# Low halves of two weight products by ScalarE and an adding DMA instead of VectorE, in a down projection by seven products

## The chip, the cores and the metric

The kernel runs on one core of one Trainium2 chip. The metric is device microseconds of one execution, the median of several runs. A run varies by about 0.1%: three runs of the kernel before took 2109.35 to 2111.09 us.

TensorE multiplies; VectorE (DVE in the profile), ScalarE (ACT) and GpSimd (POOL) prepare its operands; SyncE (SP) issues most DMAs. PEld in the profile is TensorE's load of the stationary operand, which overlaps its matmuls (PE).

## The reference

Two layers, each with two SwiGLU half-steps around a mixer of a gated linear recurrence and windowed attention. Everything is float32. What matters here is the last product of the SwiGLU, which happens four times (two per layer):

```python
def swiglu(h, w_gate, w_up, w_down):
    return (jax.nn.silu(h @ w_gate) * (h @ w_up)) @ w_down

for l in range(DEPTH):                     # 2 layers, 512 tokens, D_MODEL 1024, D_FF 2816
    h = rms_norm(x, gn[0])
    x = x + 0.5 * rms_norm(swiglu(h, w_ffn1_gate[l], w_ffn1_up[l], w_ffn1_down[l]), gn[1])
    ...
    h = rms_norm(x, gn[4])
    x = x + 0.5 * rms_norm(swiglu(h, w_ffn2_gate[l], w_ffn2_up[l], w_ffn2_down[l]), gn[5])
```

## The kernel before

**Precision.** A float32 product is made of three matmuls in a reduced float32 format. Each operand is split into a high half (the value rounded) and a low half (the rest); `mm3` adds high x high, high x low and low x high. So every weight that TensorE reads has first been split: ScalarE casts it into the high half `whi`, and the low half `wlo` is the weight minus the high half. There are two ways to make a low half:

- VectorE subtracts: `wlo = w - whi` (L286 in `quarter`, L331 in `split`).
- ScalarE writes `-w` rounded into `wlo` (L283, L328), and a DMA issued by GpSimd adds the float32 `w` onto it (L284, L329). Activations have the same two ways in `split` (L400 and L401) and `split_dma` (L410, L411, L412).

**Weights in a stream.** `Stream` holds the order in which weights are used. `load` fetches a unit of 128 x 1024 float32 into one of 4 raw buffers (`w`, tag w32), by SyncE. A unit's next load waits until all readers of the old contents are done. `split` and `quarter` make high and low halves into 6 buffers each (`whi`, `wlo`), up to three items ahead of the one in use. Whatever TensorE does is in program order; the other engines' instructions are put in order when the program is built, and each engine then runs its list strictly in that order.

**The down projection.** `down` multiplies 22 row blocks of 128 with the down weights, tokens on the output's partitions. Most of it runs in units of 256 rows (`both`). For rows 8 to 15 of the first half of the columns it uses `quarters`: a 2 x 2 block product by **seven products** of sums of the blocks instead of eight. Their order is `ORDER`: p1, p6, p2, p7, p5, p4, p3. Each product takes two weight items (index q = 0, 1), each of 128 x 1024 in two halves of 512 columns, and runs 2 items x 2 row blocks x 2 token blocks x 3 matmuls = 24 matmuls of 128x512. The matmul of one row block reads columns out of both halves of its item.

**Where the weights of a product come from.** `quarter(it)` does it: p1 and p5 read raw units 0 and 1, p2 and p4 read raw units 2 and 3, before and after these are changed; p6, p7 and p3 read sums that VectorE makes:

- p6: L267 subtracts in raw units 0 and 1 in place, L268 writes a second difference (`tt`).
- p7: L276 adds in the buffers of the second column half, and L277 adds `tt` **in place into raw units 2 and 3**, the same that p2 has read and p4 will read.

These sums are pinned: they stay in program order on VectorE. After p5 and p4 a raw unit is given back (`raw.pop`) and the next load into that buffer is queued on SyncE.

The names that recur: `x56` and `x37` in `Late` are the activations' sums for the products 5, 6 and 3, 7. The ones for product 7 and 3 are split by `late.more` through `split` (L400, L401) and `split_dma` (L410 to L412). `u2`, `u3`, `c12` and `c22` (L789) add up the products on VectorE. L799 copies p1 out of PSUM by ScalarE.

The tail of `quarter`, L278 to L286, which decides on the way of the low half:

```python
for c in range(2):
    nc.scalar.copy(it.hi[:, h[c]], w[c])                                             # L281
    if it.kind in DMAS:
        nc.scalar.mul(it.lo[:, h[c]], w[c], -1.0)                                    # L283
        nc.gpsimd.dma_start(it.lo[:, h[c]].bitcast(F32), w[c], accum_op=ALU.add)     # L284
    else:
        nc.vector.tensor_tensor(it.lo[:, h[c]], w[c], it.hi[:, h[c]].bitcast(F32), op=ALU.subtract)  # L286
```

Of the kernel before, what the change touches and what calls it, by code (L numbers as in the profile page):

```python
# [37 lines left out]
TURN = 0  # L38
LEAD = 8
ORDER = ("p1", "p6", "p2", "p7", "p5", "p4", "p3")  # L40
DMAS = ()
HEADS = (0, 4, 1, 5, 2, 6, 3, 7)


# [1 line left out]
def trunk(ctx: ExitStack, tc: tile.TileContext, xin, wall, gains, lbT, hgain, sinks, c_dist, c_mask, c_ident, out):  # L46
# [109 lines left out]
    class Stream:  # L156
# [98 lines left out]
        def quarter(self, it):  # L255
# [24 lines left out]
# [4 lines that stand above are left out]
# [1160 lines left out]
```

## Time and profile before

| | us |
|---|---|
| median of 3 runs | 2109.81 |
| lowest, highest | 2109.35, 2111.09 |
| the profiled execution, its own time | 2112.72 |
| its span, first to last instruction | 2110.9 |

The page gives busy time by engine, and the groups of instructions by line. Rows of a timeline read: start in us from the span's start, duration in us, engine, line, operation, output<-input, shape, count; in brackets the idle time of the engine before it and what ended it. A row with "x4" is four instructions one behind the other, and its duration is that of all four. Rows of one line's answer give min, median and max duration in ns, and below it who waited for that line (us, times). DMA rows give queue, packets, MB and the share of 16 DMA engines, or issues with size and us from the issue's start to landing.

The four down projections by seven products lie at about 260 to 303, 958 to 1001, 1304 to 1346 and 2002 to 2045 us.

### The profile page before, as it was taken

Reading aid. Unit: us, or ns where it says so; the run is one execution under the profiler, and the core shown is the slowest. Engines: PE = TensorE matmul, PEld = TensorE weight load, DVE = VectorE, ACT = ScalarE, POOL = GpSimd, SP = SyncE. Lnnn points to the kernel's source line nnn. Section 1 sums busy time; section 2 is a strip of 40 time slices with the busy share of each in tenths; the row PEclk is TensorE's granted clock in tenths of the full one; section 3 lists DMA queues with packets and bytes.
Section 4 is the critical chain, followed back from the end, with each engine's and each line's share of the span. In section 5 each row is a group of like instructions: output and inputs, shape, how many; then the busy total and the mean of one; then the engine's idle time right before and its main releaser. Section 6 shows DMA issues by size and latency. Waiting matters only on the chain.

```text
span 2110.9 us, 35242 instructions
## 1 busy us (share of the span) xinstructions
PE 2100.8 (100%) x13549; PEld 1874.8 (89%) x13549; DVE 1551.3 (73%) x2705; ACT 1122.6 (53%) x1899; POOL 154.6 (7%) x188
## 2 busy tenths in 40 slices
PE   9999999999999999999999999999999999999998
PEld 8899988887888999997899998898778989999987
DVE  5877886767676777789587778767686758777884
ACT  6555555446444555556355556444554445555562
POOL 0011000000000011110001110000000000111000
PEclk9999999999999999999999999999999999999999
DMA  8677653322246357774447775632122563677651
GB/s 246 152 181 182 175 167 123 101 70 65 66 110 200 127 122 182 180 195 126 151 113 176 185 179 147 190 119 91 51 71 70 135 187 108 157 182 183 179 163 47
DMA packets 148072, 298.36 MB, mean 141 GB/s; under 512 B 16992, under 2 KB 74816, under 8 KB 147904
## 3 DMA queue, kind: packets, MB, share of 16 engines
q1 hardware_dynamic: 122416, 228.16, 33.2%
q0 software_dynamic: 25344, 67.91, 18.6%
q8 instruction: 106, 1.74, 0.3%
q14 instruction: 62, 0.51, 0.1%
q10 hardware_dynamic: 144, 0.05, 0.0%
HBM read 213.43 MB, written 14.73 MB: 108 GB/s over the span
## 4 chain that ended last, share of the span: by engine, by line
PE 44%; DVE 6%; ACT 3%; issue 1%; DMA 1%; SPq 0%; ACTq 0%; DVEq 0%
PE acc L115 32%; PE aux L115 11%; ACT whi L324 1%; DVE s L401 1%; DMA w<-wall 1%; DVE wlo L286 1%; DVE wlo L331 1%; PE aux L125 1%; PE acc L125 0%; ACT s L400 0%; SPq L241 0%; DVE tt L268 0%; DVE w L267 0%; ACT m L894 0%; ACT whi L281 0%
## 5 line engine op out<-in xcount | busy, mean ns | idle before, releaser
L115 PE MATMUL acc<-s,whi 128*128 128x256 f32 (+1 forms) x4952 | 1063.0, 311 | 0.4 <-ACT whi L324 0.2
L115 PEld LDWEIGHTS acc<-s,whi 128*128 128x128 f32 x4952 | 806.2, 191 | 51.5 <-DVE s L1101 1.6
L115 PE MATMUL acc<-s,wlo 128*128 128x256 f32 (+1 forms) x2476 | 766.9, 310 | 0.1
L115 PEld LDWEIGHTS acc<-s,wlo 128*128 128x128 f32 x2476 | 472.5, 191 | 25.5 <-DVE wlo L331 0.4
L324 ACT CAST whi<-w 128x1024 fp32r<-128x1024 f32 (+1 forms) x341 | 317.1, 949 | 254.0 <-PE aux L115 95.0
L115 PE MATMUL acc<-whi,s 128*128 128x512 f32 x1264 | 414.0, 394 | 0.3 <-ACT s L400 0.2
L324 ACT CAST whi<-tt 128x1024 fp32r<-128x1024 f32 x154 | 161.6, 1049 | 342.2 <-DVE tt L318 189.2
L331 DVE TENSOR_TENSOR wlo<-w,whi 128x1024 fp32r<-128x1024 f32 (+1 forms) x181 | 218.5, 1216 | 134.0 <-ACT whi L324 133.0
L115 PEld LDWEIGHTS acc<-whi,s 128*128 128x128 f32 x1264 | 236.9, 188 | 57.6 <-issue 3.2
L331 DVE TENSOR_TENSOR wlo<-tt,whi 128x1024 fp32r<-128x1024 f32 x154 | 188.2, 1222 | 103.0 <-ACT whi L324 102.7
L115 PE MATMUL acc<-wlo,s 128*128 128x512 f32 x632 | 246.8, 391 | 1.2 <-DVE wlo L286 1.2
L329 POOL DMA_DIRECT2D wlo<-w x160 | 138.2, 865 | 1263.0 <-ACT wlo L328 869.1
L115 PE MATMUL aux<-s,whi 128*128 128x256 f32 (+1 forms) x1248 | 230.5, 285 | 0.0
L115 PE MATMUL aux<-whi,s 128*128 128x512 f32 x592 | 196.8, 390 | 0.0
L115 PEld LDWEIGHTS aux<-s,whi 128*128 128x128 f32 x1248 | 195.2, 192 | 1.1 <-issue 0.5
L115 PE MATMUL aux<-s,wlo 128*128 128x256 f32 (+1 forms) x624 | 177.6, 285 | 0.0
L115 PEld LDWEIGHTS acc<-wlo,s 128*128 128x128 f32 x632 | 118.7, 188 | 25.7 <-DVE wlo L286 2.4
L115 PEld LDWEIGHTS aux<-whi,s 128*128 128x128 f32 x592 | 111.1, 188 | 22.9
L328 ACT ACTIVATE wlo<-w 128x1024 fp32r<-128x1024 f32 (+1 forms) x160 | 130.0, 846 | 0.0
L400 ACT CAST s<-s 128x512 fp32r<-128x512 f32 (+1 forms) x164 | 88.5, 581 | 65.9 <-DVE s L459 60.6
L115 PEld LDWEIGHTS aux<-s,wlo 128*128 128x128 f32 x624 | 119.8, 192 | 0.5 <-DMA wlo<-w 0.2
L115 PE MATMUL aux<-wlo,s 128*128 128x512 f32 x296 | 115.2, 389 | 0.0
(186 smaller groups left out, 2136.6 us busy)
## 6 DMA issues: line engine op xcount, KB each, us to landing
w<-wall SPq DMA_DIRECT2D x267, 512.0 KB, 3.7
wlo<-w POOLq DMA_DIRECT2D x83, 512.0 KB, 5.5
w<-wall SPq DMA_DIRECT2D x288, 128.0 KB, 3.2
wlo<-w POOLq DMA_DIRECT2D x77, 256.0 KB, 3.3
x_d<-s SPq DMA_DIRECT2D x48, 256.0 KB, 2.1
s<-x_d SPq DMA_DIRECT2D x48, 256.0 KB, 5.3
w<-wall SPq DMA_DIRECT2D x34, 256.0 KB, 3.0
s<-wall SPq DMA_DIRECT2D x64, 128.0 KB, 3.5
```

The lines of the kernel that those rows point to most:

```text
L115: nc.tensor.matmul(o, lhsT, rhs, start=start, stop=stop)
L125: nc.tensor.transpose(o, src, ident)
L286: nc.vector.tensor_tensor(it.lo[:, h[c]], w[c], it.hi[:, h[c]].bitcast(F32), op=ALU.subtract)
L324: i = nc.scalar.copy(it.hi[:, c], w[:, c])
L328: nc.scalar.mul(it.lo[:, c], w[:, c], -1.0)
L329: nc.gpsimd.dma_start(it.lo[:, c].bitcast(F32), w[:, c], accum_op=ALU.add)
L331: nc.vector.tensor_tensor(it.lo[:, c], w[:, c], it.hi[:, c].bitcast(F32), op=ALU.subtract)
L400: nc.scalar.copy(hi, src)
L401: nc.vector.tensor_tensor(lo, src, hi.bitcast(F32), op=ALU.subtract)
```

## The change

Products p2 and p4 make their low halves by ScalarE and an adding DMA; the other five stay with VectorE. The whole diff is the list that `quarter` asks:

```diff
 ORDER = ("p1", "p6", "p2", "p7", "p5", "p4", "p3")
-DMAS = ()
+DMAS = ("p2", "p4")
 HEADS = (0, 4, 1, 5, 2, 6, 3, 7)
```

For each of the four down projections, 8 subtractions of 128x512 on VectorE (L286) are replaced by 8 scaled copies of 128x512 on ScalarE (L283) and 8 adding DMAs of 256 KB issued by GpSimd (L284).

## The prediction

> **What bounds the kernel now.** I read the busy shares first, then who waited for the two weight-splitting lines of the seven products, then one of the four places instruction by instruction.
>
> ```profile
> span 2110.9 us, 35242 instructions
> ...
> PE 2100.8 (100%) x13549; PEld 1874.8 (89%) x13549; DVE 1551.3 (73%) x2705; ACT 1122.6 (53%) x1899; POOL 154.6 (7%) x188
> ```
>
> TensorE sets the time; VectorE, with 73%, and ScalarE, with 53%, matter only where TensorE waits for them. So the question is where in the four down projections TensorE waits, and how the change moves those waits. Who waited for the high halves (L281) and for VectorE's low halves (L286):
>
> ```profile
> L286 DVE TENSOR_TENSOR wlo<-w,whi x64: 680/686/694, 243.3 to 2031.1; 128x512 fp32r<-128x512 f32 x64
> ...
>   PEld acc L115: 2.4, 4
> ...
> L281 ACT CAST whi<-w x64: 614/618/627, 241.3 to 2027.5; 128x512 fp32r<-128x512 f32 x64
> ...
>   PEld acc L115: 1.4, 4
> ```
>
> Each line stopped the weight loads four times, once per down projection: 2.4 + 1.4 = 3.8 us in all, 0.95 us a place. Both stops are in one product, shown here for the first place (TensorE's rows: the first matmul of p6, p2, p5 and p4; then the two stopped weight loads, inside p7):
>
> ```profile
> 269.10 0.39 PE L115 MATMUL aux<-whi,s 128*128 128x512 f32 x1
> 274.54 0.39 PE L115 MATMUL acc<-whi,s 128*128 128x512 f32 x1
> 286.22 0.39 PE L115 MATMUL aux<-whi,s 128*128 128x512 f32 x1
> 291.66 0.39 PE L115 MATMUL acc<-whi,s 128*128 128x512 f32 x1
> ...
> 282.80 0.19 PEld L115 LDWEIGHTS acc<-whi,s 128*128 128x128 f32 x1 [0.36 <-ACT whi L281]
> 283.60 0.19 PEld L115 LDWEIGHTS acc<-wlo,s 128*128 128x128 f32 x1 [0.61 <-DVE wlo L286]
> ```
>
> A product is 24 matmuls: 274.54 - 269.10 = 5.44 us, 0.227 us each, 2.72 us for each of its two weight items. p2 runs 274.54 to 279.98; p7 then reaches its second item at 282.7 and loses 0.95 us there. ScalarE and VectorE around it:
>
> ```profile
> 270.37 2.18 ACT L281 CAST whi<-w 128x512 fp32r<-128x512 f32 x4
> 273.41 0.62 ACT L400 CAST s<-s 128x512 fp32r<-128x512 f32 x1
> 274.45 0.63 ACT L411 ACTIVATE s<-s 128x512 fp32r<-128x512 f32 x1
> 274.98 0.61 ACT L400 CAST s<-s 128x512 fp32r<-128x512 f32 x1
> 276.96 0.62 ACT L281 CAST whi<-s 128x512 fp32r<-128x512 f32 x1 [0.31 <-DVE s L276]
> 282.66 3.22 ACT L281 CAST whi<-w 128x512 fp32r<-128x512 f32 x6
> 285.78 2.19 ACT L281 CAST whi<-s 128x512 fp32r<-128x512 f32 x4
> ...
> 271.11 2.49 DVE L286 TENSOR_TENSOR wlo<-w,whi 128x512 fp32r<-128x512 f32 x4
> 274.06 0.69 DVE L401 TENSOR_TENSOR s<-s,s 128x512 fp32r<-128x512 f32 x1 [0.47 <-ACT s L400]
> 275.63 0.69 DVE L401 TENSOR_TENSOR s<-s,s 128x512 fp32r<-128x512 f32 x1 [0.87 <-ACT s L400]
> 276.24 0.69 DVE L276 TENSOR_TENSOR s<-s,s 128x512 f32<-128x512 f32 x1
> 282.26 1.29 DVE L286 TENSOR_TENSOR wlo<-s,whi 128x512 fp32r<-128x512 f32 x2
> 284.66 4.90 DVE L286 TENSOR_TENSOR wlo<-w,whi 128x512 fp32r<-128x512 f32 x8
> ```
>
> The chain that ends in TensorE's stop, read backwards: p7's last low halves (282.26 to 283.55) close a string of VectorE work that began with the first L276 at 276.24 and has no gap. That L276 stands behind two L401, and both waited for **ScalarE's** L400 (0.47 and 0.87 us idle). So up to 275.6 ScalarE is late, not VectorE. The four subtractions that the change takes away (271.11 to 273.60) lie ahead of those idle gaps.
>
> **The change part by part.** For p2 and p4 each place loses 2 x 4 VectorE subtractions and gains 2 x 4 scaled copies on ScalarE (L283) and 2 x 4 adding DMAs of 256 KB on GpSimd (L284). In the order in which the changed program is built, TensorE's instructions are unchanged; p2's copies stand one behind each of its four L281, p4's four stand behind the first of p3's L281; the two L401 still stand ahead of the first L276.
>
> *p2's subtractions removed:* 2.49 us of VectorE. Worth 0: L401 waits for ScalarE. Below nothing they cannot go far: the cover of a gain is the 0.95 us stop in p7, 3.8 us in four places.
>
> *p2's scaled copies:* the twin is L411, which starts at 274.45 and lets L400 start at 274.98, 0.53 us. Four make 2.12 us, and all four lie between the L281 at 270.37 and the L400 that VectorE waits for. L400 goes from 274.98 to 277.10, the first L276 from 276.24 to 278.36, p7's last low halves from 283.55 to 285.67, and TensorE's restart from 283.60 to 285.72. **+2.12 us**, unless TensorE itself comes later still.
>
> *p2's adding DMAs:* their twin is the adding DMA of L412, and two rows of the weight phase show company.
>
> ```profile
> 275.38 0.86 POOL L412 DMA_DIRECT2D s<-s  x1 [4.45 <-ACT s L411]
> ...
> q0 software_dynamic: 576, 1.05, 20.2%
> ...
> s<-s POOLq DMA_DIRECT2D x4, 256.0 KB, 3.3
> ...
> 922.03 1.81 POOL L329 DMA_DIRECT2D wlo<-w  x2 [8.40 <-ACT wlo L328]
> ...
> 932.24 4.50 DMA wlo<-w
> ```
>
> GpSimd starts 0.30 us behind the scaled copy (274.45 + 0.63 to 275.38), spaces two issues by 0.95 us (1.81 - 0.86), and 256 KB land 3.3 us from the start of the issue. The queue row is of the stretch 260 to 290 us, with four such DMAs: 20.2% of 30 us / 4 = 1.5 us of all 16 DMA engines each. So DMAs issued every 1.05 us land every 1.5 us. p2's first copy ends at 270.37 + 0.52 + 0.63 = 271.52; issue 271.82; landings 275.1, 276.6, 278.1, 279.6. TensorE wants both halves of the first item at 274.77 (second matmul): 1.85 us late. The second item is wanted at 276.62 + 2.72 = 279.34, 0.28 us late. p2 ends at 282.1, p7 reaches its second item's low half at 282.1 + 2.72 + 0.23 = 285.05, still 0.67 us ahead of 285.72. So this stop of 2.1 us replaces the old one and **adds nothing** to the 2.12. The upper bound is the row at 932.24: 4.5 us for the same size among weight loads, 1.2 us more, of which 0.55 would show.
>
> [...]
>
> *Waits added, and what is queued behind.* L284 on GpSimd holds two L412 behind it: issued at 277.5 and 279.1 instead of 275.38 and 276.94, landing by 282.6; p7 wants them in its second item, 285. L277 on VectorE overwrites what p2's DMAs read, with p7's low halves behind it: it comes at 278.96 and the first landing at 275.1. Neither costs. On SyncE the third weight load waits for p4's DMAs instead of a subtraction, and every later load stands behind it: it would start about 295, land by 300, and is wanted three products after p4 starts, past 310.
>
> *p4:* its four subtractions are half of the x8 row at 284.66; nobody waits there, so 0 gained. ScalarE's x6 row moves to 284.78, the x4 row to 287.90; the scaled copies start one instruction later at 288.42, the first ends 289.05, its DMA is issued at 289.34. Alone they would land at 292.6, 294.1, 295.6, 297.1. TensorE reaches p4's first low half at 291.66 + 2.12 + 0.23 = 294.01: 0.13 late, then 296.86 against 297.1, 0.28: together 0.4 us. But weight loads stream there:
>
> ```profile
> 286.03 14.34 SPq L241 DMA_DIRECT2D w<-wall  x24
> ```
>
> They move to 288.15, and eight pieces of 128 KB share the engines with the first two DMAs. With 1.2 us (932.24) on the first pair and 0.7 more on the second from the load behind it: 1.33 + 0.98 = 2.3 us. Between 0.4 and 2.3, I take **1.3**.
>
> *The four places.* The same string stands in all: p2's L281 and the first L276 are 5.87 us apart each time.
>
> ```profile
> 969.03 2.18 ACT L281 CAST whi<-w 128x512 fp32r<-128x512 f32 x4
> 1314.56 2.18 ACT L281 CAST whi<-w 128x512 fp32r<-128x512 f32 x4
> 2012.62 2.18 ACT L281 CAST whi<-w 128x512 fp32r<-128x512 f32 x4
> ...
> 974.90 0.69 DVE L276 TENSOR_TENSOR s<-s,s 128x512 f32<-128x512 f32 x1
> 1320.43 0.69 DVE L276 TENSOR_TENSOR s<-s,s 128x512 f32<-128x512 f32 x1
> 2018.49 0.68 DVE L276 TENSOR_TENSOR s<-s,s 128x512 f32<-128x512 f32 x1
> ```
>
> **Sum:** 2.12 + 0 + 1.3 = 3.4 us a place, 13.7 us for four. TensorE is busy to the end, so nothing behind takes it back. The profiled execution took 2112.7 us (span 2110.9), the runs' median is 2109.8; 0.14% apart. On the span 2124.6; on the median **2123.5 us**. By the bounds: 4 x 2.5 = 10.1 (2119.9) to 4 x (2.12 + 0.55 + 2.3) = 19.9 (2129.7).
>
> **The rivals.**
> - *ScalarE's shift alone.* p4's DMAs land in time, because they are issued ahead of need. For it: alone they miss by 0.13 us only. Against: the stream of loads just there. 4 x 2.12 = 8.5: 2118.3 us. [...]
> - *p4's DMAs starve.* The load pieces keep the engines as long as they are issued: data until 292.5, then the pair's 3.0 us and 0.35 to land, 295.85, 1.85 late; the second pair behind four more pieces, 300.6 against 298.6, 2.0 late; with p2's 0.55, 6.5 a place: 2135.9 us. Against: at 932.24 company cost 1.2 us, not a standstill. [...]
> - *VectorE relieved, not slower.* If ScalarE had 2.1 us of room before L400, p7's string could start earlier by up to the 0.87 + 0.47 us idle, and the 0.95 us stop would go: 4 x 0.95 = 3.8, 2106.0 us. It decides once the L400 are not later than now. Against: ScalarE's rows from 270.37 on carry no idle mark before 276.96.
>
> That the change does not do what it says is out: the built order holds 32 L283 and 32 L284.
>
> **How the numbers follow.** Forecast 0.60 (2119.9 to 2129.7), ScalarE alone 0.20, starving 0.12, relieved 0.05, something unseen 0.03. About 0.2%, 4.2 us, is what a measurement of this kernel can tell from no change. The first three are slower by more: with half of the unseen, 0.93. The relieved case's ceiling of 3.8 us lies within 0.2%, so it counts as same: 0.05. Faster: 0.02. Range 2116 to 2132: it holds the forecast and the first rival, and leaves out starving and relief.
>
> **What would show it.** In the profile after: the first L276 5.87 + 2.12 = 8.0 us behind p2's first L281; weight loads stopped in p2 by the adding DMA, about 1.9 and 0.3 us; in p7 about 0.7 us from L286; in p4 0.4 to 2.3 us from the adding DMA; L277 with no wait on a DMA; nothing new behind p3. I am wrong if the distance L281 to L276 stays 5.9, if p2's stop exceeds 2.7 us, so that TensorE and not VectorE arrives last in p7, or if SyncE's held-back load stops TensorE after p3.

## The result, and the profile after

The changed kernel takes 2131.26 us (median of 4 runs, 2130.22 to 2134.47). The kernel before took 2110.09 us beside it (4 runs, 2109.35 to 2111.09). The ratio is 1.010, 95% interval 1.0088 to 1.0111: slower by 21.2 us, where 13.7 were forecast (3.4 a place).

The head of the page after:

```profile
span 2129.7 us, 35376 instructions
...
PE 2104.0 (99%) x13549; PEld 1875.9 (88%) x13549; DVE 1532.9 (72%) x2673; ACT 1138.4 (53%) x1931; POOL 182.5 (9%) x220
```

Against the page before, VectorE lost 18.4 us of busy time, ScalarE gained 15.8 and GpSimd 27.9. TensorE has 3.2 us more, though its instructions are the same; where that comes from is shown under the clock.

To find the 21 us, I took the time from each product's first matmul to the next product's first matmul out of the trace. A "place" is one of the four down projections. Products 1, 6, 5 and 3 take 5.44 us in both kernels in every place. The others (us, places 1 to 4):

| | p2 | p7 | p4 |
|---|---|---|---|
| before | 5.44, 5.44, 5.44, 5.44 | 6.24, 6.20, 6.23, 6.20 | 5.44, 5.44, 5.44, 5.44 |
| after | 9.16, 7.73, 7.75, 7.54 | 5.44, 6.00, 6.02, 5.99 | 9.55, 8.13, 7.89, 8.50 |

The sum of the seven products over the four places went from 155.4 to 176.7 us, 21.3 more. So the loss lies in p2, p7 and p4; what follows kept its time (for instance 55.9 us from p3's first matmul to the end of the down projection in the first three places, in both kernels). The spans of the two profiled executions are only 18.8 us apart (2110.9 and 2129.7): outside the seven products this pair differs by 2.5 us the other way, 1.0 of it ahead of the first place, where nothing is changed. Single executions of the changed kernel lie some 4 us apart, so that 21.3 comes so close to 21.2 is partly luck.

**p2 and p7.** The second place, which is undisturbed: ScalarE and VectorE from p2's first cast to p7's first sum (timeline view of after).

```profile
974.38 0.62 ACT L281 CAST whi<-w 128x512 fp32r<-128x512 f32 x1
974.90 0.62 ACT L283 ACTIVATE wlo<-w 128x512 fp32r<-128x512 f32 x1
...
979.50 0.62 ACT L400 CAST s<-s 128x512 fp32r<-128x512 f32 x1
...
980.15 0.69 DVE L401 TENSOR_TENSOR s<-s,s 128x512 fp32r<-128x512 f32 x1 [4.95 <-ACT s L400]
981.72 0.69 DVE L401 TENSOR_TENSOR s<-s,s 128x512 fp32r<-128x512 f32 x1 [0.87 <-ACT s L400]
982.32 0.68 DVE L276 TENSOR_TENSOR s<-s,s 128x512 f32<-128x512 f32 x1
```

From the first L281 to the first L276 it is now 982.32 - 974.38 = 7.94 us; it was 5.87. VectorE, freed of four subtractions, stands idle for 4.95 us instead and waits for ScalarE.

TensorE in the same place: the first matmuls of p2, p5, p4 and p3, and the stops between them, picked out of the timeline:

```profile
978.60 0.39 PE L115 MATMUL acc<-whi,s 128*128 128x512 f32 x1
980.93 0.47 PE L115 MATMUL acc<-wlo,s 128*128 128x512 f32 x1 [1.94 <-DMA wlo<-w]
989.69 0.50 PE L115 MATMUL acc<-wlo,s 128*128 128x512 f32 x1 [0.24 <-DVE wlo L286]
992.34 0.39 PE L115 MATMUL aux<-whi,s 128*128 128x512 f32 x1
997.78 0.39 PE L115 MATMUL acc<-whi,s 128*128 128x512 f32 x1
999.92 0.47 PE L115 MATMUL acc<-wlo,s 128*128 128x512 f32 x1 [1.76 <-DMA wlo<-w]
1003.30 0.47 PE L115 MATMUL acc<-wlo,s 128*128 128x512 f32 x1 [0.37 <-DMA wlo<-w]
1005.90 0.39 PE L115 MATMUL acc<-whi,s 128*128 128x512 f32 x1
...
983.69 0.19 PEld L115 LDWEIGHTS acc<-wlo,s 128*128 128x128 f32 x1 [0.20 <-issue]
989.69 0.19 PEld L115 LDWEIGHTS acc<-wlo,s 128*128 128x128 f32 x1 [0.61 <-DVE wlo L286]
```

The bracket is only the part of a wait in which no earlier matmul still ran: from 978.60 to 980.93 TensorE loses 2.10 us against its usual 0.227, of which the bracket counts 1.94. The 0.61 us in p7 are the weight load's; the matmul behind it counts 0.24 of them.

**The adding DMAs.** The last row of L284's answer over the four DMAs of p2 in the second place, and over the four of p4 there (us from issue to landing: min, median, max):

```profile
DMA to landing us min/median/max: 3.3/4.1/4.6
...
DMA to landing us min/median/max: 4.4/6.5/8.2
```

p2's are issued 1.04 us apart and land 3.3, 5.0, 6.4 and 7.8 us behind the first issue; forecast were 3.3, 4.8, 6.3 and 7.8. p4's are issued 0.55 us apart and land 4.4, 6.5, 8.2 and 9.9 us behind the first. At the spacing of 1.5 us that p2's show, four of them would land at 3.3, 4.8, 6.3 and 7.8. So beside the weight loads each comes later, by 1.1 us for the first to 2.1 us for the fourth. (With all loads held back, below, the four do land 3.4, 4.9, 6.4 and 7.7 us behind the first issue.) What runs beside them (DMA view of after, 285 to 300 us; queue, packets, MB, share of the 16 engines):

```profile
q0 software_dynamic: 576, 1.05, 39.0%
q1 hardware_dynamic: 1713, 1.56, 36.9%
```

q0 is the four adding DMAs, q1 the weight loads. 39.0% of 15 us is 5.9 us of all engines for four adding DMAs, 1.5 us each, as for the four L412 of before with no weight loads beside them (37.9% of the 16 us from 266 to 282). What they took beyond that fell into time in which the engines carried loads too (36.9%). In the second place both queues move data in every single microsecond from 995 to 1002 us.

**The clock.** The first place lost 1.5 us more in p2 and 1.4 more in p4 than the mean of the others. Windows view of after: span of the window, its length, busy us (count) of PE, PEld, DVE, ACT and POOL, granted clock, DMA share, GB/s.

```profile
272.66:276.07 3.41, 1.56 (x7) 1.02 (x6) 0.69 (x1) 3.41 (x8) 1.72 (x2) 1.00 1.04 174
276.07:279.48 3.41, 3.41 (x9) 2.67 (x8) 2.92 (x5) 2.51 (x5) 1.72 (x2) 0.50 1.04 177
293.14:296.55 3.41, 1.16 (x6) 0.68 (x5) 3.04 (x5) 0.99 (x1) 0.00 (x0) 1.00 1.12 223
296.55:299.96 3.41, 3.41 (x10) 2.63 (x9) 0.63 (x2) 0.12 (x1) 0.00 (x0) 0.50 0.77 227
979.21:982.62 3.41, 1.69 (x7) 1.43 (x8) 1.60 (x3) 3.41 (x7) 1.46 (x2) 1.00 1.10 186
982.62:986.03 3.41, 3.41 (x16) 2.69 (x15) 3.41 (x7) 1.36 (x3) 0.86 (x1) 1.00 1.00 169
```

For 3.41 us behind the first place's stops in p2 and in p4, TensorE's granted clock was half (0.50). Its matmuls then start 0.427 us apart instead of 0.227; eight of them lose 1.6 us. Twice 1.6 is TensorE's extra busy time of 3.2 us. What it cost was less where a later wait shrank by it: in p2 and p7 together the first place lost 0.9 us more than the others, since p7 then had no stop. The second place's stop of p2, 1.94 us by its bracket where the first place's has 1.85, is followed by full clock (1.00). The trace of before has no such stretch ahead of its last 6 us.

Not all of the 1.4 us in p4 is the clock. In the first place p4's adding DMAs landed 5.9 to 9.7 us behind their own issue, against 4.4 to 8.6 us in the other three, and TensorE's first stop there was 2.4 us instead of 1.9 to 2.1. Why they landed later is open.

### The profile page after: what moved, and what is told of

Its sections match the earlier page's. It is cut to its first block, busy times and chain, and to the rows that moved or that the text cites. A ratio compares the mean times of both kernels' runs of the same rounds, so it can differ in the third digit from the quotient of the medians.

```text
span 2129.7 us, 35376 instructions
## 1 busy us (share of the span) xinstructions
PE 2104.0 (99%) x13549; PEld 1875.9 (88%) x13549; DVE 1532.9 (72%) x2673; ACT 1138.4 (53%) x1931; POOL 182.5 (9%) x220
## 4 chain that ended last, share of the span: by engine, by line
PE 73%; DVE 7%; ACT 4%; DMA 3%; issue 2%; SPq 1%; POOL 0%; DVEq 0%; ACTq 0%; POOLq 0%
PE acc L115 54%; PE aux L115 17%; DMA wlo<-w 2%; DVE wlo L286 1%; PE aux L125 1%; DVE s L401 1%; DMA w<-wall 1%; ACT whi L324 1%; ACT s L400 1%; PE acc L125 1%; SPq L241 1%; ACT whi L281 1%; DVE tt L268 0%; DVE w L267 0%; DVE s L276 0%
## 5 line engine op out<-in xcount | busy, mean ns | idle before, releaser
L115 PEld LDWEIGHTS acc<-wlo,s 128*128 128x128 f32 x632 | 119.3, 189 | 46.2 <-issue 21.3
L400 ACT CAST s<-s 128x512 fp32r<-128x512 f32 (+1 forms) x164 | 88.4, 580 | 65.8 <-DVE s L459 60.6
L401 DVE TENSOR_TENSOR s<-s,s 128x512 fp32r<-128x512 f32 (+1 forms) x164 | 99.4, 640 | 31.0 <-ACT s L400 30.7
```

The lines of the kernel that those rows point to most:

```text
L115: nc.tensor.matmul(o, lhsT, rhs, start=start, stop=stop)
L400: nc.scalar.copy(hi, src)
L401: nc.vector.tensor_tensor(lo, src, hi.bitcast(F32), op=ALU.subtract)
```

## The experiments

Each run was compared with the kernel before on the same chip. The first four shared one set of runs (before 2110.21 us), the next three another (2110.73), the last two a third (2110.39).

### ScalarE's scaled copies alone

```diff
                 else:
+                    if it.kind == "p2":
+                        nc.scalar.mul(it.lo[:, h[c]], w[c], -1.0)
                     nc.vector.tensor_tensor(it.lo[:, h[c]], w[c], it.hi[:, h[c]].bitcast(F32), op=ALU.subtract)
```

> No adding DMA at all: the four scaled copies of p2 are put on ScalarE between its casts, and VectorE then overwrites what they wrote with the subtraction of before. Theory (ScalarE's four copies alone hold back the L400, and by them p7): p2 stays 5.44 us, p7 goes from 6.2 to 8.3 us in each place, 8.5 us in all, plus 1.7 us for each fall of TensorE's clock that the 3.1 us stop brings. Rival (the landing of p2's DMAs sets the loss, the copies are free): p7 stays 6.2 us and the time stays within 1 us of before.

Measured: 2118.41 us (2117.53 to 2119.43), ratio 1.0040 (1.0025 to 1.0055), 8.2 us more. p2 takes 6.14 to 6.33 us, p7 7.39 to 7.40, p4 5.44; no stretch of half clock. The second place (timeline; L286 of before is L288 here, L400 is L402):

```profile
969.04 0.61 ACT L281 CAST whi<-w 128x512 fp32r<-128x512 f32 x1
...
970.22 0.69 DVE L288 TENSOR_TENSOR wlo<-w,whi 128x512 fp32r<-128x512 f32 x1 [0.36 <-ACT wlo L287]
...
974.82 0.69 DVE L403 TENSOR_TENSOR s<-s,s 128x512 fp32r<-128x512 f32 x1 [0.78 <-ACT s L402]
976.38 0.69 DVE L403 TENSOR_TENSOR s<-s,s 128x512 fp32r<-128x512 f32 x1 [0.87 <-ACT s L402]
976.99 0.69 DVE L276 TENSOR_TENSOR s<-s,s 128x512 f32<-128x512 f32 x1
```

L281 to L276 is 7.95 us, as in the changed kernel, with no adding DMA at all. p2 and p7 together cost 1.9 to 2.1 us more a place. That p2 shares in it was not expected: the subtraction overwrites what the copy wrote and so waits for it (0.36 us at L288), which the changed kernel does not do.

### p2 alone, and p4 alone

The change with one product in the list: `DMAS = ("p2",)`, then `DMAS = ("p4",)`.

> Only p2 goes by ScalarE and the adding DMA. Theory (two waits side by side, the later one counts): p2 7.6 to 7.8 us, p7 6.0 us, p4 5.44 us, so 2.1 us a place and 8.4 us in all, plus 1.7 us for each fall of the clock. Rival (the two costs add up): p7 8.3 us beside p2 7.6 us, 17 us in all.

> Only p4 goes by ScalarE and the adding DMA. Theory (p4's late landing is its own, by weight loads beside it): p2 5.44, p7 6.2, p4 7.9 to 8.5 us, 2.4 to 3.1 us a place, 9.8 to 12 us in all plus 1.7 us for each fall of the clock. Rival (p4 is late because p2's copies pushed ScalarE back): p4 below 6.1 us, under 3 us in all.

Measured, p2 alone: 2119.76 us, ratio 1.0047 (1.0032 to 1.0062), 9.6 us more. p2 takes 9.31, 7.74, 7.47, 7.52 and p7 5.44, 6.01, 5.99, 5.98. In places 2 to 4 the two cost 1.8 to 2.1 us together, no more than the copies alone: the DMAs' own stop of 2.1 us in p2 is hidden. The first place has one stretch of half clock behind this stop and costs 3.1 us; with the copies alone, where TensorE has no such stop in p2, there was none.

p4 alone: 2121.81 us, ratio 1.0054 (1.0037 to 1.0071), 11.6 us more. p7 stays at 6.12 to 6.26, p4 takes 7.94, 8.17, 8.10, 8.59: 2.5 to 3.2 us a place. 9.6 + 11.6 = 21.2 us, which is the whole change; each of the two is known to some 3 us, so the times by product carry this better than the sum. The two products' costs add, and p4's is the larger.

### p4 alone, its neighbours' loads held back

All four raw buffers are given back only at p4's second item. Pinned one-column copies by GpSimd read the last low half and the raw buffers; the next loads wait for them. In the first version the copies read the first two raw buffers:

```diff
-            if it.kind in ("p5", "p4"):
-                self.raw.pop(it.u)
-                self.freed += 1
+            if it.kind == "p4" and q == 1:
+                j = small([P, 1], "gate", 2)
+                pin(nc.gpsimd.tensor_copy(j, it.lo[:, D - 1 : D].bitcast(F32)))
+                for i in range(4):
+                    if i < 2:
+                        pin(nc.gpsimd.tensor_copy(j, self.raw[it.base + i][:, :1]))
+                    self.raw.pop(it.base + i)
+                    self.freed += 1
```

In the second, all four:

```diff
-                    if i < 2:
-                        pin(nc.gpsimd.tensor_copy(j, self.raw[it.base + i][:, :1]))
+                    pin(nc.gpsimd.tensor_copy(j, self.raw[it.base + i][:, :1]))
```

> p4 alone, and the loads into the four raw buffers held back until p4's last adding DMA has landed, by three one-column copies on GpSimd. Theory (the loads take the DMA engines from the adding DMAs): p4's DMAs land 3.3, 5.0, 6.4 and 7.8 us behind the first issue, as p2's did; p4 5.7 to 6.2 us. The held loads may bring a stop of their own behind p3. Rival (the four DMAs are issued too late and too close, the loads do not matter): p4 stays at 7.5 us or more.

> p4 alone by ScalarE and adding DMAs; all four raw buffers are given back only when the last of p4's four adding DMAs has landed (one-column GpSimd copies read the last low half and all four raw units), so that no weight load shares the engines with any of the four. Theory (the 1.2 to 1.4 us that were left with the loads held to the second landing came from the fourth DMA, which still met them): the fourth lands 5.0 us behind its issue instead of 6.5, the second item's stop goes, p4 takes 5.7 to 6.0 us, 0.3 to 0.6 over 5.44, and the time is about 2112 us. Rival (the adding DMAs alone are late, loads or none): p4 stays at 6.5 us, 2114 to 2116 us. The later loads may show behind p3.

Measured, two buffers: 2115.44 us, ratio 1.0024 (1.0014 to 1.0035); p4 takes 6.86, 6.55, 6.51, 6.53. The hold was only partial, since a load into one of the other two buffers started when the second DMA had landed (in the second place at 990.83, 4.9 us behind the first issue). All four: 2113.46 us, ratio 1.0014 (1.0005 to 1.0023); p4 takes 6.49, 5.96, 5.95, 5.97. p4's four DMAs in the second place, for p4 alone, with two buffers held, and with four:

```profile
DMA to landing us min/median/max: 4.9/6.6/8.1
```

```profile
DMA to landing us min/median/max: 3.3/4.7/6.5
```

```profile
DMA to landing us min/median/max: 3.4/4.7/5.9
```

And the order of things with all four held (timeline, second place):

```profile
985.05 3.52 POOL L284 DMA_DIRECT2D wlo<-w  x4 [9.42 <-DVE wlo L286]
...
994.05 16.19 SPq L241 DMA_DIRECT2D w<-wall  x32
...
990.03 0.47 PE L115 MATMUL acc<-wlo,s 128*128 128x512 f32 x1 [0.15 <-DMA wlo<-w]
```

The loads start at 994.05, behind the last landing (985.05 + 7.7). One stop of p4 is left, 0.15 us by its bracket, and p4 loses 0.5 us in three of the four places, close to the 0.4 that the prediction gave for the DMAs alone. The fourth landed 5.9 us behind its issue; the 5.0 written down before the run was wrong arithmetic (at 1.5 us a DMA and issues 0.6 us apart it is 3.3 + 3 x 0.9 = 6.0). So the loads cost p4 about 2.1 us a place (mean of p4 alone 8.20, mean held 6.09).

### The changed kernel once more

> The changed kernel once more, for a second profile. Theory (the clock's windows run free of the kernel, and a fall needs a stop of some 2 us inside one of them): the half-clock stretches of 3.41 us stand at other products, or there are one or three of them instead of two, and p2 and p4 without one take 7.5 to 7.8 and 7.9 to 8.5 us as before. Rival (the falls belong to the first place, for instance to what runs there): again two, again in p2 and p4 of the first place, 9.2 and 9.6 us.

Measured: 2131.99 us (2129.33 to 2134.23), ratio 1.0100 (1.0086 to 1.0114). The profiled run has three stretches of half clock, in p2 of place 1 (from 277.28 us), in p4 of place 3 and in p4 of place 4 (from 2052.21). The second of them, and p2 of place 2 for comparison (windows view):

```profile
1345.64:1349.05 3.41, 1.61 (x8) 1.04 (x7) 3.08 (x5) 0.59 (x1) 0.00 (x0) 1.00 1.12 223
1349.06:1352.47 3.41, 3.41 (x10) 2.67 (x9) 0.25 (x2) 1.10 (x2) 0.00 (x0) 0.50 0.84 238
...
977.01:980.42 3.41, 1.63 (x7) 1.40 (x8) 1.54 (x3) 3.41 (x7) 1.51 (x2) 1.00 1.08 183
980.42:983.83 3.41, 3.41 (x16) 2.64 (x16) 3.41 (x7) 1.42 (x3) 0.86 (x1) 1.00 1.00 171
```

p4 of place 1, which had 9.55 us, now has 7.44; p4 of places 3 and 4 have 9.09 and 9.19. The starts are whole multiples of 3.413 us apart in both profiles: (296.55 - 276.07) / 6 = 3.413 in the first, (1349.06 - 277.28) / 314 = 3.4133 and (2052.21 - 1349.06) / 206 = 3.4133 here. The rival, that the falls belong to the first place, is out, since two of the three lie elsewhere. One thing is not settled: p2 of the first place fell in every profile that has its stop (both of the changed kernel, p2 alone, and the last kernel below), p2 of the other places in none of the first three. What separates all these cases is how much TensorE ran in the window ahead: 1.61 us or less and the clock fell, 1.63 and it did not. The two figures differ by 0.02 us, no more than the windows' edges are known to (each is read to 0.01), so in these profiles the limit lies at about 1.6 us.

p4 of places 1 and 2, at full clock here, lost 2.00 and 2.71 us.

### The activations' splits, earlier or in another order

Both kernels try to take away the old stop in p7 by relieving ScalarE's order. The first moves all of p7's splits to the start of the seven products; the second leaves them where they were and puts both L400 ahead of the L410 and L411.

```diff
-        late.more(2)
+        late.more(4)
...
-        late.more(4)
```

> The kernel before, with product 7's activations split at the start of the seven products instead of between p6 and p2, so that the two L400 and L401 stand ahead of p2's four L281 on ScalarE. Theory (p7's stop comes from ScalarE being late with L400, by four L281 of 2.18 us): the first L276 follows directly behind p2's four L286, p7 falls from 6.20-6.24 to 5.44 us, 4 x 0.78 = 3.1 us, about 2107.0 us. Rival (the four L281 of p2 are now late instead): the stop moves into p2, 0.3 to 0.8 us there and a part in p7, nothing gained or slightly slower, 2110 to 2112 us.

Measured: 2111.45 us, ratio 1.0003 (0.9994 to 1.0012). Nothing gained; p7 takes 6.33, 6.20, 5.95, 6.37. VectorE ahead of p7's first sum (timeline, second place; p2 starts at 971.37):

```profile
969.68 0.69 DVE L401 TENSOR_TENSOR s<-s,s 128x512 fp32r<-128x512 f32 x1 [0.71 <-ACT s L400]
...
971.77 1.29 DVE L286 TENSOR_TENSOR wlo<-w,whi 128x512 fp32r<-128x512 f32 x2 [0.79 <-ACT whi L281]
972.98 0.69 DVE L276 TENSOR_TENSOR s<-s,s 128x512 f32<-128x512 f32 x1
```

VectorE waits for ScalarE as before, now at L286 for L281 instead of at L401 for L400. The first L276 is 1.61 us behind p2's start; before, it was 974.90 - 973.23 = 1.67. ScalarE has the same copies to do in either order.

```diff
             for i in range(len(self.x37), n):
                 self.src[self.k0 + 4 + i] = split(self.src[self.k0 + 4 + i])
+            for i in range(len(self.x37), n):
                 self.x37.append(pair_split(self.t[i], split_dma))
```

> The kernel before, with one loop of the activations' splitting cut in two: both L400 first, then the four L410 and L411 with their adding DMAs, so that between the two L400 on ScalarE one L410 and one L411 (1.04 us) are gone. The run with the splits moved ahead of p2 gained nothing, because ScalarE still had the same copies to do before p7's first L276. Theory (what counts is ScalarE's number of copies ahead of the last one that VectorE needs before the first L276): the first L276 comes 1.0 us earlier behind p2's first L281, 4.9 instead of 5.87 us, p7 falls from 6.2 to 5.44-5.6 us, 2.4 to 3.1 us in four places, about 2107.5 to 2108.2 us. Rival (p7's own L281, now behind the two L411, holds VectorE's string instead): p7 stays near 6.0 us, under 1 us in all.

> The changed kernel with the same order of the splits. Theory (in p7 of the changed kernel VectorE's string arrives last, 0.56 us behind TensorE; p2's stop is the adding DMAs' alone): p2 stays at 7.5 to 7.8 us, p7 falls from 6.0 to 5.44, p4 stays at 7.9 to 8.5, about 2.2 us less than the changed kernel, 2129 us, but for the clock falls (1.7 us each). Rival (the L412 behind p2's DMAs or TensorE's own lateness sets p7): p7 stays at 6.0 us.

Measured on the kernel before: 2110.10 us, ratio 1.0000 (0.9991 to 1.0009); p7 takes 5.64, 5.68, 5.99, 6.13, 1.4 us less in the four places by the profile. The times do not show it, but their interval (1.9 us to either side) could not tell it from nothing.

```profile
966.86 2.17 ACT L281 CAST whi<-w 128x512 fp32r<-128x512 f32 x4
...
971.75 0.69 DVE L276 TENSOR_TENSOR s<-s,s 128x512 f32<-128x512 f32 x1
...
979.11 0.19 PEld L115 LDWEIGHTS acc<-wlo,s 128*128 128x128 f32 x1 [0.37 <-DVE wlo L286]
```

L281 to L276 is 4.89 us, as expected, but p2's first L281 itself slid from 4.20 to 3.76 us ahead of p2 (p2 starts at 970.62 here, at 973.23 before), since a L410 and a L411 of the first pair of splits now stand ahead of it. About half of the 1.0 us was given back there.

On the changed kernel: 2132.30 us, ratio 1.0104 (1.0090 to 1.0118). It is not 2 us faster, as expected, but the same. p7 fell to 5.44 in all places; p2 rose to 10.62, 10.44, 11.79, 11.07; p4 fell to 7.20, 5.59, 5.62, 5.68. The second place:

```profile
974.79 0.60 ACT L281 CAST whi<-w 128x512 fp32r<-128x512 f32 x1
...
975.17 0.86 POOL L412 DMA_DIRECT2D s<-s  x1 [0.70 <-ACT s L411]
976.22 0.86 POOL L284 DMA_DIRECT2D wlo<-w  x1 [0.18 <-issue]
...
993.17 3.52 POOL L284 DMA_DIRECT2D wlo<-w  x4 [8.89 <-ACT wlo L283]
...
981.80 0.47 PE L115 MATMUL acc<-wlo,s 128*128 128x512 f32 x1 [3.11 <-DMA wlo<-w]
```

p2's casts start 3.5 us ahead of p2 instead of 4.2, and a L412 goes out just ahead of p2's DMAs. The stop in p2 becomes 3.1 us by its bracket, and in all four places half clock follows. p4 then starts 2.0 us later against its own DMAs, which are issued as before: p4's first is issued 6.7 us before TensorE wants the second (993.17 against 999.86), where the changed kernel has 4.7 (993.32 against 998.01). The second lands 6.5 us behind the first issue there. With a lead of 6.7 us p4 loses 0.15 to 0.24 us in places 2 to 4. (In place 1 it loses 1.8; its four DMAs landed 5.9 to 9.3 us behind their own issue there.)

No kernel tried here is measurably faster than the one before.

## Why the prediction was right in direction and low in size

The time lies in the range (2116 to 2132), but by 0.7 us, and above the sum of the prediction's own bounds (2129.7): no case that the prediction priced gives it, and that it stays inside is partly luck. Three of the eight single executions of the changed kernel took more than 2132. The forecast was 13.7 us, the loss 21.2. By steps:

- **p2's subtractions are worth nothing.** Right: VectorE waits 4.95 us for ScalarE where they stood.
- **Four scaled copies shift p7's string by 2.12 us.** Right. L281 to L276 went from 5.87 to 7.94 us. p2 and p7 together cost 2.09, 2.10 and 1.89 us in places 2 to 4. The copies alone cost the same.
- **p2's adding DMAs add nothing.** Right outside the clock, and shown by the run with the copies alone beside the run with p2 alone. The landings of 3.3, 5.0, 6.4, 7.8 us are those worked out from L412 and the queue's row. p2 lost 2.3 us and p7 0.6 in the second place, where 1.85 + 0.28 and 0.67 were named. But it is this stop in p2 behind which the clock fell in the first place.
- **L277 and SyncE's held-back load cost nothing.** Right: L277's answer after has no wait, and what lies behind p3 kept its time.
- **p4 costs 0.4 to 2.3 us, taken as 1.3.** This is the step that failed, in size. It measured 2.69, 2.45 and 3.06 us in places 2 to 4, above the upper bound; 2.73 on average instead of 1.3 makes 5.7 us over four places. (In the second profile p4 lost 2.00 and 2.71 us where the clock stayed full.) The lead was right (4.67 us forecast to the second low half, 4.69 measured), the DMAs alone were right (0.4 forecast, 0.5 with the loads held), the place and the cause were right. Wrong was the price of company: at most 1.2 us for a pair, taken from a single DMA among loads, and between the bounds of 0.4 and 2.3 the prediction took the middle without a reason. In p4's burst of the second place it grew: 1.1, 1.7, 1.9, 2.1 us from the first to the fourth. The second DMA decides when p4 can go on, and it had 1.7. So TensorE's first stop in p4 took 1.9 to 2.1 us in places 2 to 4 (0.13 to 1.33 by the prediction); the second, 0.3 to 0.8, kept its bounds (0.28 to 0.98).
- **The clock was not thought of.** Two stretches of half clock in the profiled run, both in place 1. It costs 2.92 us in p2 and p7 and 4.11 in p4, against 2.03 and 2.73 on average in the other three: 2.3 us more for both, most of it the clock's, some of it the later landing of p4's DMAs there.

Together: 4 x 2.03 + 4 x 2.73 + 2.3 = 21.3 us.

Why the single DMA was no fair price shows in SyncE's rows beside it, in before, and beside p4's DMAs of the second place, in after:

```profile
933.35 6.62 SPq L241 DMA_DIRECT2D w<-wall  x11
...
992.10 8.15 SPq L241 DMA_DIRECT2D w<-wall  x9
```

The loads beside the single DMA (issued at 932.24) were issued 1.1 us behind it, and the trace has no packet of a load between 933 and 935 us, while most of its own data moved. p4's first DMA (993.32) was issued 1.2 us behind its loads, and their packets ran beside all four.

Of the rivals, ScalarE's shift alone fell with the stops in p4. "Starving" had the right place and the right cause, at too high a price (6.5 us a place; without the clock it was 4.8): the measured size of p4 lies between the forecast and it. The queue's rows show the two kinds of transfer side by side in the same 15 us, 39.0% and 36.9% of the engines, so the adding DMAs were slowed, not stopped: 3.3 us from issue to landing alone, 4.4 to 8.2 in company in the second place. The relieved VectorE did not show, and the two kernels that tried for its 3 us found at most half of it in the profile and nothing clear of noise in the time.

## What to carry to other kernels

When work moves to a DMA, compare its lead (from its issue to the first use) with its landing in the traffic that runs there, for the DMA in the burst that is needed, not the first: here 4.7 us of lead stood against 3.3 us alone and 6.5 us beside weight loads. Before an engine is relieved, look at what its next idle mark waits for; here VectorE waited for ScalarE, and the change gave ScalarE the work. Where TensorE stops for some 2 us in one piece, look at the granted clock behind the stop as well: here eight matmuls lost 1.6 us each time that it was 0.50 for 3.41 us, of which about half was hidden by a later wait in p2 and p7, and behind stops of like length it stayed at 1.00 where they left 1.63 us or more of matmuls in the window of 3.41 us ahead.

## What the runs showed of the hardware

**Behind stops of some 2 us the granted clock was 0.50 for 3.41 us in some places and 1.00 in others.** In the two profiles of the changed kernel the stretches of half clock start on a grid of 3.413 us (6 steps between the two of the first, 314 and 206 between the three of the second) whose position against the kernel differs from execution to execution: in the first place the stretch began 2.5 us behind p2's first matmul in one profile of the changed kernel, 3.7 us in the other. Over the profiles of the runs with stops long enough, I took TensorE's busy time in the grid window ahead, at full clock, from the windows view. Ten stretches began behind windows with 0.81, 1.01, 1.16, 1.41, 1.44, 1.46, 1.54, 1.56, 1.57 and 1.61 us of matmuls; behind windows with 1.63 (twice), 1.64, 1.66, 1.67, 1.69, 1.70 and more the clock stayed full. On that grid the whole first trace of the changed kernel has one further window with less than 1.64 us, at its end (2122.68 to 2126.09, 1.28 us), with a clock of 0.50 behind it. A pair in two neighbouring windows of the last kernel, with the half clock that follows:

```profile
2030.49:2033.90 3.41, 1.63 (x8) 1.01 (x6) 0.00 (x0) 3.41 (x8) 2.79 (x4) 1.00 1.04 175
2033.91:2037.32 3.41, 1.46 (x6) 1.23 (x7) 3.15 (x6) 3.37 (x8) 1.14 (x2) 1.00 1.10 185
2037.33:2040.74 3.41, 3.41 (x10) 2.64 (x9) 3.41 (x6) 1.62 (x3) 0.57 (x1) 0.50 1.04 180
```

So among these windows half clock followed each that had 1.61 us of matmuls or less at full clock (47% of 3.41 us), and none that had 1.63 or more. In the first profile p2's stop of the first place lay whole in its window (273.93 to 275.78, window from 272.66 to 276.07); that of the second place began 0.22 us ahead of one (978.99, window from 979.21). The same kernel had two stretches in one execution and three in the other. One stretch, in the last kernel, lasted two windows (6.83 us); TensorE was busy for 2.50 us of its first, at half clock, so the limit is not the same number there.

**Beside weight loads each adding DMA of a burst of four landed later, the fourth by most.** In the second place p4's four of 256 KB landed 4.4 to 8.2 us behind their own issue beside the loads, and 3.4 to 5.9 with the loads held back; one alone took 3.3 (L412, before). Against landings at 3.3 us and every 1.5 us after it, the first was 1.1 us late and the fourth 2.1.
